# Column-major products of a four-layer decoder: two passes of 512 and 256 columns in place of three of 256

## The chip, the cores and the metric

The kernel runs as one program on one core of a Trainium2 chip. The metric is the device time of one execution in microseconds (us); a smaller number is better. The engines named below are PE (TensorE, matmuls; its weight loads have a row of their own, PEld), DVE (VectorE), ACT (ScalarE), POOL (GpSimd) and SP (SyncE, which issues the weight transfers).

## The reference

256 tokens of 1024 features pass four layers. The mixer of layer i is number i mod 3: HGRN2 (0), mLSTM (1), sliding-window attention (2), so HGRN2 comes twice, in layers 0 and 3.

```python
for layer in range(DEPTH):
    g = norm_gains[layer]
    h = x + 0.5 * swiglu(rmsnorm(x, g[0]), w_ffn_gu[layer, 0], w_ffn_down[layer, 0])
    xn = rmsnorm(h, g[1])
    ...
    h = h + mix
    h = h + 0.5 * swiglu(rmsnorm(h, g[2]), w_ffn_gu[layer, 1], w_ffn_down[layer, 1])
    gate = jax.nn.sigmoid(rmsnorm(h, g[3]) @ w_ple_gate[layer])
    x = h + gate * (p[layer] @ w_ple_proj[layer])
```

`mix` is the mixer of the layer on `xn`. `swiglu(x, w_gu, w_down)` is `(silu(g) * u) @ w_down` with `g, u` the two halves of `x @ w_gu`. `w_gu` is 1024 x 5632 and `w_down` 2816 x 1024, so the eight SwiGLU blocks hold most of the work.

## The kernel before, in words

Everything is in 32 bits. Each operand of a large product is split into two parts of 12 bits, `hi` (a cast on ACT) and `lo = x - hi` (a subtraction on DVE), and a product is the sum of three matmuls: hi.hi, hi.lo and lo.hi. Features lie on the 128 partitions, so a "feature tile" is 128 features by 256 tokens. There are 8 such tiles of the residual (KT) and 22 of the SwiGLU's middle (FT).

Weights stream from memory in units of 128 x 1024 values, two to a transfer, in the order that `weight_plan` writes out. `unit()` splits a unit on ACT and DVE (L238, L239) three units before it is used (AHEAD_UNITS), into one of six `wh` and one of six `wl` buffers. A cast therefore waits until PE has left the unit that had the buffer before.

`gemm_cols` is the column-major product: weights are the stationary operand (128 columns of a unit), activations of 256 tokens move through. For each of a unit's eight column tiles c, `mm_w` issues three matmuls of 256 columns, each with its own weight load: wh on xh, wh on xl, wl on xh (L251 to L253). Two column tiles share a PSUM bank of 512 values. The k loop is outside, so all banks of a group are done at once. The gate and up product of a SwiGLU runs in groups of four gate and four up tiles, the down product and the embedding gate (`ple`) in two halves of four tiles, the HGRN2 projection and the query and key projection of mLSTM in groups of eight. `gemm_rows` is the token-major product (L260 to L262): activations are stationary, weights move, 512 columns at a time. What reads a finished bank is DVE: in `ffn` a product by the tokens' norm `rb` (L393), SiLU on ACT, a product by the up part (L395) and a split; in `ple` L461 to L464. `push` splits a finished pair of residual tiles into `xh`, `xl` for the next product.

The work of the mixers (HGRN2's levels of decays, attention, softmax) and of the norm runs "later": generators that `tick` advances by one step per share of a unit, so their instructions stand between the products' in each engine's queue. The norm's `rb` comes after some five units of the next product. PSUM's eight banks are five for `acc`, two for `mis` and one for `out` (attention's and HGRN2's outputs). The order of the instructions on an engine is settled when the program is built, not at run time; each engine works its queue in that order.

Of the kernel before, what the change touches and what calls it, by code (L numbers as in the profile page):

```python
# [52 lines left out]

def weight_plan():
    plan = []

    def gu(l, f):
        for j in range(0, FT, 4):
            n = min(4, FT - j)
            c0, w = j * P, n * P  # L60
            cols = [(c0, w), (FF + c0, w)]
            if n == 4:
                for k in range(KT):
                    plan.append([("w_ffn_gu", (l, f), k, cols)])
            else:
                for k in range(0, KT, 2):
                    plan.append([("w_ffn_gu", (l, f), k, cols), ("w_ffn_gu", (l, f), k + 1, cols)])
# [4 lines left out]

    def halves(name, idx, nk):
        for hf in range(2):
            pairs(name, idx, hf * 512, range(nk))
# [10 lines left out]
    def ffn(l, f):  # L86
        gu(l, f)
        halves("w_ffn_down", (l, f), FT)

    for l, kind in enumerate(kinds()):  # L90
        j = (l // 3,)
        ffn(l, 0)
        if kind == 0:
            for hg in range(2):
                for k in range(KT):
                    plan.append([("hg_w_in", j, k, [(D + hg * 512, 512), (hg * 512, 512)])])
# [3 lines left out]
        elif kind == 1:  # L100
            full("ml_w_qkvo", j, 0)
# [11 lines left out]
        halves("w_ple_gate", (l,), KT)  # L113
# [3 lines left out]
class Kern:  # L117
    def __init__(self, ctx, tc, a):
# [29 lines left out]
    def s512(self, name):  # L148
        return self.tmp.tile([P, 512], F32, tag="s512", name=self.nm(name), bufs=6)

    def bank(self):
        return self.acc.tile([P, 512], F32, tag="acc", name=self.nm("acc"))
# [4 lines left out]
    def obank(self):  # L157
        return self.out.tile([P, 512], F32, tag="out", name=self.nm("out"))

# [21 lines left out]
    def settle(self, gen=None):  # L181
        """Emits all that waits, or all up to the end of gen, or until gen() holds."""
# [6 lines left out]
    def unit(self):  # L189
        """The next unit's two parts; units up to AHEAD_UNITS later are split before work that comes after."""  # L190
# [4 lines left out]
    def make_unit(self):  # L195
# [3 lines left out]
        if n % 2 == 0:  # L199
# [9 lines left out]
            elif n < 8:  # L209
                for i in range(2):  # L210
                    nc.sync.dma_start(out=self.raw[:, i, :], in_=src[:, i, :])
                if n < 6:
                    self.load_x(1 + n // 2)
            else:
                nc.sync.dma_start(out=self.raw, in_=src)
        raw = self.raw[:, n % 2, :]
        wh = self.wh.tile([P, U], F32R, tag="wh", name=self.nm("wh"))
        wl = self.wl.tile([P, U], F32R, tag="wl", name=self.nm("wl"))
        segs = self.plan[n]
        if segs[0][0] == "ml_w_out":  # L220
            # the rows' gains
# [11 lines left out]
        if n in (1, 3, 5):  # L233
            self.push(1 + n // 2)
# [11 lines left out]
    def mm_w(self, ps, w, c, x, first, last, opens):  # L246
        """ps[128 columns of w, tokens] += w[:, c:c+128].T @ x"""
# [7 lines left out]
    def mm_x(self, ps, w, c, n, x, t, first, last):  # L255
        """ps[tokens of tile t, n columns of w] += x[:, t].T @ w[:, c:c+n]"""
# [7 lines left out]
    def gemm_cols(self, x, ncol=U):  # L264
        """Column-major product over one group of ncol columns: banks of two column tiles."""
        nk = len(x)
        banks = [self.bank() for _ in range(ncol // 256)]
        per = U // ncol
        for k0 in range(0, nk, per):
            w = self.unit()  # L270
            for i in range(per):
                k = k0 + i
                for c in range(ncol // P):
                    self.mm_w(banks[c // 2][:, (c % 2) * T:(c % 2 + 1) * T], w, i * ncol + c * P, x[k],
                              k == 0, k == nk - 1, c % 2 == 0)
                self.tick(1.0 / per)
        return banks

    def gemm_rows(self, x, ncol=U):
        """Token-major product over one group of ncol columns: [t][512 columns], of half a bank if ncol is 256."""  # L280
        nk = len(x)
        if ncol == 256:
            b = self.bank()
            banks = [[b[:, t * 256:(t + 1) * 256]] for t in range(NT)]
        else:
            banks = [[self.bank() for _ in range(ncol // 512)] for _ in range(NT)]
        w = min(ncol, 512)
        per = U // ncol
        for k0 in range(0, nk, per):
            u = self.unit()  # L290
            for i in range(per):
                k = k0 + i
                for t in range(NT):
                    for n, b in enumerate(banks[t]):
                        self.mm_x(b, u, i * ncol + n * w, w, x[k], t, k == 0 and (w == 512 or t == 0), k == nk - 1)
# [888 lines left out]
```

## Time and profile before

| what | value |
|---|---|
| median of 3 runs (lowest, highest) | 2152.64 us (2149.27, 2152.68) |
| span of the profiled execution, first to last instruction | 2147.6 us |
| what lies around that span, against the median | 5.0 us |
| PE busy, PE instructions | 99% of the span, 17061 |
| DVE busy, ACT busy | 64%, 50% |
| granted TensorE clock, mean | 0.999 of 2.4 GHz |

The profile gives one execution on the chip. It does not print a run time for that execution; the three timed runs lie 1.7 to 5.1 us above its span. A matmul's row shows a start and a duration; consecutive matmuls overlap, so the spacing of their starts, and not the duration, is what one costs in a stream.

### The profile page before, as it was taken

The page shows a single profiled execution, that of the slowest core. Times are in us where ns is not written, and L with a number is a line of the kernel's source. Part 1 is how long each engine was busy: PE and PEld are TensorE (multiplying, and loading weights), DVE is VectorE, ACT ScalarE, POOL GpSimd, SP SyncE. Part 2 cuts the span into 40 slices and gives each one's busy share as a digit, 9 for nine tenths or more (in the row PEclk, how much of TensorE's full clock was granted, in tenths as well). Part 3 has the DMA queues.
Part 4 walks back from the last instruction along what each step waited for, and adds up shares of the span by engine and source line. Part 5 has one row for each costly group of instructions (what it writes and reads, how often), then busy time and mean ns, then how long its engine had stood idle before and what let it go on. Part 6 is the DMA issues. An engine that isn't in the chain of part 4 may idle for free.

```text
span 2147.6 us, 39752 instructions
## 1 busy us (share of the span) xinstructions
PE 2126.2 (99%) x17061; PEld 2078.8 (97%) x17061; DVE 1380.6 (64%) x1831; ACT 1083.4 (50%) x1442; POOL 49.1 (2%) x84
## 2 busy tenths in 40 slices
PE   8999999999999999999999999999999999999998
PEld 8999989999999989999999997899999999899998
DVE  6656986555855566665676567665576558966565
ACT  5444655443644456544454447544464445564443
POOL 2000000000000000000000001000000000000000
PEclk9999999999999999999999999999999999999999
DMA  7554344455455544454545452355554553445452
GB/s 287 180 193 177 118 160 180 179 191 181 177 184 189 180 156 163 182 190 177 188 178 184 179 195 99 123 188 181 182 183 186 177 187 129 157 155 196 177 180 77
DMA packets 54033, 372.84 MB, mean 174 GB/s; under 512 B 6368, under 2 KB 7264, under 8 KB 9568
## 3 DMA queue, kind: packets, MB, share of 16 engines
q1 hardware_dynamic: 53568, 370.21, 47.9%
q8 instruction: 133, 2.18, 0.4%
q14 instruction: 44, 0.36, 0.0%
q10 hardware_dynamic: 288, 0.09, 0.0%
HBM read 369.23 MB, written 1.05 MB: 172 GB/s over the span
## 4 chain that ended last, share of the span: by engine, by line
PE 95%; DVE 4%; ACT 1%; issue 0%; POOL 0%; DMA 0%; POOLq 0%; ACTq 0%; DVEq 0%
PE acc L252 28%; PE acc L253 28%; PE acc L251 28%; PE acc L260 2%; PE acc L261 2%; PE acc L262 2%; PE mis L625 1%; DVE slab L632 1%; PE mis L1005 1%; DVE slab L638 1%; DVE wl L239 0%; PE mis L368 0%; DVE slab L640 0%; PE mis L613 0%; DVE slab L597 0%
## 5 line engine op out<-in xcount | busy, mean ns | idle before, releaser
L239 DVE TENSOR_TENSOR wl<-wraw,wh 128x1024 fp32r<-128x1024 f32 (+1 forms) x693 | 846.1, 1222 | 620.9 <-ACT wh L238 619.5
L238 ACT CAST wh<-wraw 128x1024 fp32r<-128x1024 f32 (+1 forms) x693 | 723.7, 1046 | 950.0 <-PE acc L252 836.4
L251 PE MATMUL acc<-xh,wh 128*128 128x256 f32 x3392 | 965.0, 285 | 6.6 <-ACT xh L242 6.1
L252 PE MATMUL acc<-xl,wh 128*128 128x256 f32 x3392 | 963.0, 284 | 0.5 <-DVE xl L243 0.5
L253 PE MATMUL acc<-xh,wl 128*128 128x256 f32 x3392 | 962.5, 284 | 0.0
L251 PEld LDWEIGHTS acc<-xh,wh 128*128 128x128 f32 x3392 | 652.9, 193 | 7.0 <-ACT xh L242 6.1
L252 PEld LDWEIGHTS acc<-xl,wh 128*128 128x128 f32 x3392 | 653.0, 193 | 0.8 <-DVE xl L243 0.8
L253 PEld LDWEIGHTS acc<-xh,wl 128*128 128x128 f32 x3392 | 652.9, 193 | 0.0
L252 PE MATMUL acc<-slab,wh 128*128 128x256 f32 x1664 | 468.5, 282 | 0.0
L253 PE MATMUL acc<-slab,wl 128*128 128x256 f32 x1664 | 468.1, 281 | 0.0
L251 PE MATMUL acc<-slab,wh 128*128 128x256 f32 x1664 | 467.8, 282 | 0.1
L252 PEld LDWEIGHTS acc<-slab,wh 128*128 128x128 f32 x1664 | 313.8, 189 | 1.2 <-issue 1.0
L251 PEld LDWEIGHTS acc<-slab,wh 128*128 128x128 f32 x1664 | 313.6, 189 | 1.3 <-issue 0.8
L253 PEld LDWEIGHTS acc<-slab,wl 128*128 128x128 f32 x1664 | 313.6, 188 | 0.5 <-issue 0.3
L260 PE MATMUL acc<-wh,xh 128*128 128x512 f32 (+1 forms) x272 | 103.3, 380 | 0.0
L262 PE MATMUL acc<-wh,xl 128*128 128x512 f32 (+1 forms) x272 | 101.1, 372 | 0.0
L261 PE MATMUL acc<-wl,xh 128*128 128x512 f32 (+1 forms) x272 | 100.8, 370 | 0.0
L393 DVE TENSOR_TENSOR gs<-acc,rb 128x512 f32<-128x512 f32 x88 | 60.5, 688 | 57.7 <-PE acc L253 57.3
L394 ACT ACTIVATE gs<-gs 128x512 f32<-128x512 f32 x88 | 55.4, 630 | 19.6 <-DVE gs L393 19.5
L395 DVE TENSOR_TENSOR gs<-gs,acc 128x512 f32<-128x512 f32 x88 | 59.9, 682 | 1.2 <-ACT gs L394 0.7
L262 PEld LDWEIGHTS acc<-wh,xl 128*128 128x128 f32 x272 | 51.8, 190 | 8.7 <-issue 0.3
L260 PEld LDWEIGHTS acc<-wh,xh 128*128 128x128 f32 x272 | 51.8, 191 | 8.5 <-issue 1.3
(224 smaller groups left out, 1281.8 us busy)
## 6 DMA issues: line engine op xcount, KB each, us to landing
wraw<-in_w_all SPq DMA_DIRECT2D x346, 1024.0 KB, 4.8
wraw<-in_w_all SPq DMA_DIRECT2D x7, 512.0 KB, 7.4
pt<-in_pT SPq DMA_DIRECT2D x4, 256.0 KB, 5.0
h<-in_xT SPq DMA_DIRECT2D x3, 256.0 KB, 6.4
wraw<-in_w_all SPq DMA_DIRECT2D x2, 256.0 KB, 4.5
outT<-h SPq DMA_DIRECT2D x2, 256.0 KB, 2.1
outT<-h SPq DMA_DIRECT2D x4, 128.0 KB, 1.7
h<-in_xT SPq DMA_DIRECT2D x2, 128.0 KB, 4.5
```

The costliest lines, as they stand in the source:

```text
L238: self.nc.scalar.copy(out=hi, in_=src)
L239: self.nc.vector.tensor_tensor(out=lo, in0=src, in1=hi.bitcast(F32), op=ALU.subtract)
L251: mm(ps, wh[:, cs], xh, start=first and opens, stop=False, skip_group_check=True)
L252: mm(ps, wh[:, cs], xl, start=False, stop=False, skip_group_check=True)
L253: mm(ps, wl[:, cs], xh, start=False, stop=last, skip_group_check=True)
L260: mm(ps, xh[:, ts], wh[:, cs], start=first, stop=False, skip_group_check=True)
L261: mm(ps, xh[:, ts], wl[:, cs], start=False, stop=False, skip_group_check=True)
L262: mm(ps, xl[:, ts], wh[:, cs], start=False, stop=last, skip_group_check=True)
L393: nc.vector.tensor_tensor(out=self.two(gs), in0=self.two(g), in1=self.bc(rb), op=ALU.mult)
L394: nc.scalar.activation(gs, gs, AF.Silu)
L395: nc.vector.tensor_tensor(out=gs, in0=gs, in1=u, op=ALU.mult)
L625: nc.tensor.matmul(ps[:, i * P:(i + 1) * P], ks[:, c], qs[:, c], start=True, stop=True)
```

## The change

The parts xh and xl of a feature tile now lie side by side in one tile `x` of 512 columns. One matmul of 512 columns takes wh through both; a second of 256 columns adds wl on xh to the second half of the same bank. A column tile so fills a bank, the sum of whose halves is the result: `fold` copies one half on ACT and adds the other on DVE.

```diff
-    def mm_w(self, ps, w, c, x, first, last, opens):
...
+    def mm_t(self, ps, w, c, x, first, last):
+        wh, wl = w
+        mm = self.nc.tensor.matmul
+        cs = slice(c, c + P)
+        mm(ps, wh[:, cs], x, start=first, stop=False, skip_group_check=True)
+        mm(ps[:, T:], wl[:, cs], x[:, :T], start=False, stop=last, skip_group_check=True)
...
+def tile_order(n, nk, head):
+    return [(c, k) for k in range(nk) for c in range(head)] + [(c, k) for c in range(head, n) for k in range(nk)]
...
+    def gemm_tiles(self, x, n, head, done):
+        nk = len(x)
+        ps = {}
+        for i, (c, k) in enumerate(tile_order(n, nk, head)):
+            if i % 8 == 0:
+                w = self.unit()
+            if c // 2 not in ps:
+                ps[c // 2] = self.pair()
+            p = ps[c // 2]
+            self.mm_t(p[:, (c % 2) * 512:(c % 2 + 1) * 512], w, (i % 8) * P, x[k], k == 0, k == nk - 1)
+            if k == nk - 1:
+                done(c, p)
+            self.tick(0.125)
...
+    def fold(self, ps, out, c=0, n=2):
+        nc = self.nc
+        p4 = ps.rearrange("p (c h t) -> p c h t", c=2, h=2)[:, c:c + n]
+        o3 = out.rearrange("p (c t) -> p c t", t=T)
+        nc.scalar.copy(out=o3, in_=p4[:, :, 1, :])
+        nc.vector.tensor_tensor(out=o3, in0=p4[:, :, 0, :], in1=o3, op=ALU.add)
+        return out
```

The products that use it are gate and up (44 column tiles, `head` 4), down (8 tiles of 22 k, `head` 2), the embedding gate, both HGRN2 projections and mLSTM's queries and keys (8 tiles each, `head` 4). The first `head` tiles run with k outside; after them each tile runs all its k in a row. `weight_plan` orders the weights to match. The sums, counts and sizes of the transfers stay. `gemm_cols` with `mm_w` stays for the embedding projection, and `mm_w` in `out_proj` and mLSTM's gates.

```diff
-        self.acc = pool("acc", 5, space=PSUM)
+        self.acc = pool("acc", 3, space=PSUM)
         self.mis = pool("mis", 2, space=PSUM)
-        self.out = pool("out", 1, space=PSUM)
...
-                nc.vector.tensor_tensor(out=self.two(gs), in0=self.two(g), in1=self.bc(rb), op=ALU.mult)
+            t = self.fold(ps, self.s512("gu"))
...
+            nc.vector.tensor_tensor(out=self.two(g), in0=self.two(g), in1=self.bc(rb), op=ALU.mult)
...
-        def gates(hg, banks):
-            g, k, q, f = [self.slab() for _ in range(4)]
-            for i in range(2):
-                s = slice(i * 512, (i + 1) * 512)
-                nc.vector.tensor_tensor(out=self.two(f[:, s]), in0=self.two(banks[i]), in1=self.bc(rb), op=ALU.mult)
-                nc.vector.tensor_tensor(out=self.two(q[:, s]), in0=self.two(banks[2 + i]), in1=self.bc(rb), op=ALU.mult)
...
+        def gates(hg, f, q):
+            g, k = self.slab(), self.slab()
+            for x in (f, q):
+                x4 = x.rearrange("p (k t) -> p k t", t=T)
+                nc.vector.tensor_tensor(out=x4, in0=x4, in1=self.bc(rb, 4), op=ALU.mult)
```

The `acc` tiles are now three pairs of banks, and `out`'s work goes to `mis`. The tiles of `x`, `wh` and `wl` take 1028 values per partition instead of 512 or 1024, and the pool of 512-column scratch tiles has seven buffers instead of six. At the start of the program the four pairs of the input are loaded and pushed with units 0 to 3 instead of 0, 1, 3 and 5, since a head of four tiles takes two k from each unit.

On PE, in the gate and up product of layer 1, the order before is this (three matmuls per column tile, `acc` a bank of two column tiles, `xh` and `xl` one k):

```order
L251 MATMUL acc_6197<-xh_6097,wh_6201 128x256
L252 MATMUL acc_6197<-xl_6098,wh_6201 128x256
L253 MATMUL acc_6197<-xh_6097,wl_6202 128x256
L251 MATMUL acc_6197<-xh_6097,wh_6201 128x256
L252 MATMUL acc_6197<-xl_6098,wh_6201 128x256
L253 MATMUL acc_6197<-xh_6097,wl_6202 128x256
L251 MATMUL acc_6198<-xh_6097,wh_6201 128x256
L252 MATMUL acc_6198<-xl_6098,wh_6201 128x256
L253 MATMUL acc_6198<-xh_6097,wl_6202 128x256
```

In the change the product after its head stands so on PE (`acc` a pair of banks, `x` a pair of feature tiles, hence two k of one column tile on each):

```order
L275 MATMUL acc_5170<-x_4978,wh_5086 128x512
L276 MATMUL acc_5170<-x_4978,wl_5087 128x256
L275 MATMUL acc_5170<-x_4978,wh_5086 128x512
L276 MATMUL acc_5170<-x_4978,wl_5087 128x256
L275 MATMUL acc_5170<-x_4987,wh_5086 128x512
L276 MATMUL acc_5170<-x_4987,wl_5087 128x256
L275 MATMUL acc_5170<-x_4987,wh_5086 128x512
L276 MATMUL acc_5170<-x_4987,wl_5087 128x256
```

Three rows of 256 columns became two, of 512 and 256, and the same column tile goes on from k to k where the row before moved to the next tile.

On DVE, in the second HGRN2 projection of layer 0, before: L590 and L591 read the finished banks and multiply by `rb`, and L632 are steps of the first four heads' levels.

```order
L590 TENSOR_TENSOR slab_2943<-acc_2604,rb_2316 128x512
L632 TENSOR_TENSOR tot_2869<-tot_2824 128x16
L632 TENSOR_TENSOR slab_2584<-slab_2584,tot_2824 128x16x32
L591 TENSOR_TENSOR slab_2942<-acc_2606,rb_2316 128x512
L632 TENSOR_TENSOR slab_2585<-slab_2585,tot_2824 128x16x32
L632 TENSOR_TENSOR slab_2584<-slab_2584,tot_2869 128x8x64
L590 TENSOR_TENSOR slab_2943<-acc_2605,rb_2316 128x512
L591 TENSOR_TENSOR slab_2942<-acc_2607,rb_2316 128x512
L632 TENSOR_TENSOR slab_2585<-slab_2585,tot_2869 128x8x64
L597 TENSOR_SCALAR slab_2940<-slab_2940,omlb,lb 128x256 x2
```

In the change, at the same place: L300 are the additions of `fold`, L693 and L698 steps of the levels, L244 a weight split, L657 the products by `rb`, now on 1024 columns that lie in SBUF.

```order
L693 COPY_PREDICATED slab_1840<-mask_279,mis_2171 128x512
L698 TENSOR_TENSOR tot_2185<-tot_2143 128x64
L300 TENSOR_TENSOR slab_2067<-acc_2073,slab_2067 128x512
L693 COPY_PREDICATED slab_1841<-mask_279,mis_2177 128x512
L698 TENSOR_TENSOR slab_1846<-slab_1846,tot_2143 128x64x8
L698 TENSOR_TENSOR slab_2053<-slab_2053,tot_2143 128x64x8
L300 TENSOR_TENSOR slab_2067<-acc_2099,slab_2067 128x512
L244 TENSOR_TENSOR wl_2218<-wraw_2191,wh_2217 128x1024
...
L300 TENSOR_TENSOR slab_2068<-acc_2297,slab_2068 128x512
L657 TENSOR_TENSOR slab_2067<-slab_2067,rb_1839 128x1024
L657 TENSOR_TENSOR slab_2068<-slab_2068,rb_1839 128x1024
```

Four additions of 512 columns came in between the levels' steps, and two rows of 1024 columns follow where four of 512 stood.

On PE, at the seam from the embedding gate of layer 0 to the gate and up product of layer 1, the change puts this (`x_4978` to `x_4996` are pairs 0 to 2 of the residual's parts, `x_5051` pair 3, `acc_5062` and `acc_5071` the head's four tiles, `acc_5170` the pair after the head):

```order
L275 MATMUL acc_5170<-x_4987,wh_5086 128x512
L276 MATMUL acc_5170<-x_4987,wl_5087 128x256
L275 MATMUL acc_5170<-x_4996,wh_5086 128x512
L276 MATMUL acc_5170<-x_4996,wl_5087 128x256
L275 MATMUL acc_5170<-x_4996,wh_5086 128x512
L276 MATMUL acc_5170<-x_4996,wl_5087 128x256
L275 MATMUL acc_5062<-x_5051,wh_5058 128x512
L276 MATMUL acc_5062<-x_5051,wl_5059 128x256
L275 MATMUL acc_5062<-x_5051,wh_5058 128x512
L276 MATMUL acc_5062<-x_5051,wl_5059 128x256
L275 MATMUL acc_5071<-x_5051,wh_5058 128x512
L276 MATMUL acc_5071<-x_5051,wl_5059 128x256
```

The last two k of the head wait for pair 3, and six k of the next column tile were moved ahead of them.

## Rows read from the trace of the kernel before

**Rows 1.** the page: span, busy us by engine, granted clock, chain that ended last.

```profile
span 2147.6 us, 39752 instructions
...
PE 2126.2 (99%) x17061; PEld 2078.8 (97%) x17061; DVE 1380.6 (64%) x1831; ACT 1083.4 (50%) x1442; POOL 49.1 (2%) x84
...
PEclk9999999999999999999999999999999999999999
...
PE 95%; DVE 4%; ACT 1%; issue 0%; POOL 0%; DMA 0%; POOLq 0%; ACTq 0%; DVEq 0%
```

**Rows 2.** groups by line: count, busy us, mean ns, idle us before, releaser.

```profile
L251 PE MATMUL acc<-xh,wh 128*128 128x256 f32 x3392 | 965.0, 285 | 6.6 <-ACT xh L242 6.1 <-DVE gs L461 0.5
...
L239 DVE TENSOR_TENSOR wl<-wraw,wh 128x1024 fp32r<-128x1024 f32 (+1 forms) x693 | 846.1, 1222 | 620.9 <-ACT wh L238 619.5
L238 ACT CAST wh<-wraw 128x1024 fp32r<-128x1024 f32 (+1 forms) x693 | 723.7, 1046 | 950.0 <-PE acc L252 836.4 <-PE acc L262 45.9 <-issue 30.3
...
L251 PE MATMUL acc<-slab,wh 128*128 128x256 f32 x1664 | 467.8, 282 | 0.1
...
L395 DVE TENSOR_TENSOR gs<-gs,acc 128x512 f32<-128x512 f32 x88 | 59.9, 682 | 1.2 <-ACT gs L394 0.7
...
L446 ACT COPY pw<-acc 128x512 f32<-128x512 f32 x16 | 9.2, 588 | 1.4 <-PE acc L253 1.0
```

**Rows 3.** timeline of PE, a gate and up product, 104 rows: start, duration us.

```profile
399.81 0.28 PE L252 MATMUL acc<-xl,wh 128*128 128x256 f32 x1
...
412.17 0.28 PE L253 MATMUL acc<-xh,wl 128*128 128x256 f32 x1
```

**Rows 4.** timeline of PE, a down product, 106 rows.

```profile
524.82 0.28 PE L252 MATMUL acc<-slab,wh 128*128 128x256 f32 x1
...
537.20 0.28 PE L252 MATMUL acc<-slab,wh 128*128 128x256 f32 x1
```

**Rows 5.** timeline of PE, token-major product of layer 0, 13 consecutive 512-column rows.

```profile
261.16 0.40 PE L260 MATMUL acc<-wh,xh 128*128 128x512 f32 x1
...
263.89 0.39 PE L260 MATMUL acc<-wh,xh 128*128 128x512 f32 x1
```

**Rows 6.** windows in layer 0's HGRN2 mixer: busy us (instructions) by engine, clock.

```profile
225.00:230.00 5.00, 5.00 (x44) 5.00 (x43) 4.97 (x6) 4.97 (x9) 0.00 (x0) 1.00 0.00 0
260.00:265.00 5.00, 5.00 (x27) 4.28 (x27) 5.00 (x7) 4.96 (x11) 0.00 (x0) 1.00 0.47 143
...
300.00:305.00 5.00, 5.00 (x27) 4.27 (x26) 1.85 (x2) 3.38 (x5) 0.00 (x0) 1.00 0.59 215
```

**Rows 7.** timeline of DVE, start of the HGRN2 gates of layer 0.

```profile
224.15 0.68 DVE L590 TENSOR_TENSOR slab<-acc,rb 128x512 f32<-128x512 f32 x1
...
239.37 1.22 DVE L632 TENSOR_TENSOR slab<-slab,tot 128x1024 f32<-128x1024 f32 x1
```

**Rows 8.** timeline of ACT and DVE, end of the embedding gate of layer 0.

```profile
556.46 0.37 ACT L370 COPY rb<-mis 128x256 f32<-128x256 f32 x1 [1.35 <-PE mis L368]
556.85 1.28 ACT L462 ACT_TABLE_LOAD   x1
...
570.85 1.69 DVE L243 SCALAR_TENSOR_TENSOR xl<-h,gains,xh 128x256 fp32r<-128x256 f32 x4 [0.20 <-ACT xh L242]
```

**Rows 9.** timeline of ACT, PE and DVE around the last product.

```profile
2131.03 0.37 ACT L370 COPY rb<-mis 128x256 f32<-128x256 f32 x1 [6.92 <-PE mis L368]
...
2139.84 0.39 PE L251 MATMUL acc<-xh,wh 128*128 128x256 f32 x1 [0.52 <-DVE gs L461]
...
2143.00 0.42 DVE L461 TENSOR_TENSOR gs<-acc,rb 128x256 f32<-128x256 f32 x1 [1.79 <-PE acc L253]
...
2144.43 0.42 DVE L464 TENSOR_TENSOR h<-gs,h 128x256 f32<-128x256 f32 x1
```

**Rows 10.** waits: who waited for whom, us in total, times, longest.

```profile
ACT wh L238 <- PE acc L252: 836.4, 497, 5.6
```

**Rows 11.** the tile out: one operation's duration ns, min/median/max.

```profile
L239 DVE TENSOR_TENSOR slab<-out,slab x8: 393/420/426, 1319.1 to 1364.3; 128x256 fp32r<-128x256 f32 x8
```

More of the change, by code (lines that the diff above doesn't have):

```diff
@@ L87, in ffn @@
         gu(l, f)
-        halves("w_ffn_down", (l, f), FT)
+        tiles("w_ffn_down", (l, f), run(0, KT), FT, 2)
     for l, kind in enumerate(kinds()):
@@ L94, in weight_plan @@
             for hg in range(2):
-                for k in range(KT):
-                    plan.append([("hg_w_in", j, k, [(D + hg * 512, 512), (hg * 512, 512)])])
+                tiles("hg_w_in", j, run(D + hg * 512, 4) + run(hg * 512, 4), KT, 4)
             full("hg_w_in", j, 2 * D)
@@ L100, in weight_plan @@
         elif kind == 1:
-            full("ml_w_qkvo", j, 0)
+            tiles("ml_w_qkvo", j, run(0, 8), KT, 4)
             full("ml_w_qkvo", j, D)
@@ L112, in weight_plan @@
         ffn(l, 1)
-        halves("w_ple_gate", (l,), KT)
+        tiles("w_ple_gate", (l,), run(0, KT), KT, 4)
     return plan
@@ L148, in s512, with pair, banks @@
     def s512(self, name):
-        return self.tmp.tile([P, 512], F32, tag="s512", name=self.nm(name), bufs=6)
-    def bank(self):
-        return self.acc.tile([P, 512], F32, tag="acc", name=self.nm("acc"))
+        return self.tmp.tile([P, 512], F32, tag="s512", name=self.nm(name), bufs=7)
+    def pair(self):
+        return self.acc.tile([P, 1024], F32, tag="acc", name=self.nm("acc"))
+    def banks(self, n):
+        ps = [self.pair() for _ in range(n // 2)]
+        return [ps[i // 2][:, (i % 2) * 512:(i % 2 + 1) * 512] for i in range(n)]
     def misc(self):
         return self.mis.tile([P, 512], F32, tag="mis", name=self.nm("mis"))
-    def obank(self):
-        return self.out.tile([P, 512], F32, tag="out", name=self.nm("out"))
     def later(self, gen):
@@ L281, in gemm_rows @@
         nk = len(x)
[L282 to L286, printed above, removed]
         w = min(ncol, 512)
+        banks = self.banks(NT * ncol // w)
+        banks = [[b[:, :w] for b in banks[t * (ncol // w):(t + 1) * (ncol // w)]] for t in range(NT)]
         per = U // ncol
@@ L401, in ffn @@
[L401 to L410 removed]
+        aT = [None] * FT
@@ new lines, in ffn, with gate @@
+        todo = deque()
+        def gate(j, g, u):
+            nc.vector.tensor_tensor(out=self.two(g), in0=self.two(g), in1=self.bc(rb), op=ALU.mult)
+            nc.scalar.activation(g, g, AF.Silu)
+            nc.vector.tensor_tensor(out=g, in0=g, in1=u, op=ALU.mult)
+            s = self.slab(F32R)
+            s4 = s.rearrange("p (c h t) -> p c h t", c=2, h=2)
+            self.split(s4[:, :, 0, :], s4[:, :, 1, :], self.two(g))
+            for i in range(2):
+                aT[2 * j + i] = s[:, i * 512:(i + 1) * 512]
@@ new lines, in flush, with gated @@
+        def flush():
+            while todo:
+                gate(*todo.popleft())
+        def gated(c, ps):
+            if c % 2 == 0:
+                return
+            j = c // 4
+            t = self.fold(ps, self.s512("gu"))
+            if c % 4 == 1:
+                self.g = t
+                return
+            todo.append((j, self.g, t))
+            if len(todo) > 1:
+                self.settle(norm)
+            if norm not in self.bg:
+                flush()
+        self.gemm_tiles(x, 2 * FT, 4, gated)
@@ new lines, in ffn, with added @@
+        self.settle(norm)
+        flush()
+        self.start_norm(self.gain(l, 2 * f + 1))
+        def added(c, ps):
+            if c % 2 == 0:
+                return
+            j = c // 2
+            y = self.fold(ps, self.s512("y"))
+            nc.vector.tensor_tensor(out=self.two(y), in0=self.two(y), in1=self.bc(rb), op=ALU.mult)
+            nc.vector.scalar_tensor_tensor(out=self.h[j], in0=y, scalar=0.5, in1=self.h[j],
+                                           op0=ALU.mult, op1=ALU.add)
+            self.push(j)
@@ L415, in out_proj @@
         self.start_norm(self.gain(l, 2))
-        banks = [self.bank() for _ in range(4)]
+        banks = self.banks(4)
         for k0 in range(0, KT, 2):
```

177 lines of the change are left out of this document (78 added, 99 removed).

## The prediction

> **What bounds the kernel now.** I read the page first. PE is busy for 99% of the span of 2147.6 us, 95% of the chain that ended last is PE's, and the granted clock is at its upper level, 2.4 GHz, in every slice [rows 1]. So PE's queue sets the time nearly everywhere, and the question is what one matmul costs in a stream. Neither the busy time nor the mean duration of 285 ns [rows 2] tells that, since rows overlap; the spacing of starts in the timeline does.
>
> In a gate and up product 104 rows start between 399.81 and 412.17 us: 12.36 us over 103 steps, 120.0 ns for a matmul of 256 columns [rows 3]. In a down product it is 12.38 us over 105 steps, 117.9 ns [rows 4]. In a token-major product, matmuls of 512 columns start 2.73 us apart over 12 steps, 227.5 ns, with a weight load for each as well [rows 5]. Two of 256 columns cost 240 and one of 512 costs 227.5, so a pass costs some 12 to 13 ns beside its columns (256 columns at 2.4 GHz are 106.7 ns, 512 are 213.3).
>
> Then the groups by line and the waits say who could get in the way. DVE splits a unit in 1.22 us and ACT casts it in 1.05 [rows 2], while PE uses it in 24 x 0.120 = 2.88 us; ACT's longest wait, 836 us in sum, is for PE to release a buffer [rows 10]. So both have time in the large products. The windows show the exception: in the HGRN2 mixer DVE is busy 5.00 of 5 us from about 225 to 300 us, and falls back to 1.85 after that [rows 6].
>
> **What the change removes.** A column tile and k cost three passes of 256 before, and one of 512 and one of 256 now. The columns stay at 768, one pass goes. There are 3392 such triples on `x` and 1664 on slabs [rows 2]; 256 of the latter are `out_proj`'s (8 x 8 in four layers) and stay, so 1408 belong to the down products. Of the 3392, 128 are the second HGRN2 projections (64 in each of two layers), which run inside the DVE-bound stretch; I count nothing for them. For the other 3264: 360.0 - (227.5 + 120.0) = 12.5 ns each, 40.8 us. For the down products: 353.7 - (227.5 + 117.9) = 8.3 ns each, 11.7 us. Together 52.5 us.
>
> The trace holds no 512-column pass with weights as the stationary operand, nor one that alternates with 256. The nearest row is the token-major stream, and I take it for both. Bounds: if the 512-column pass also profits from what makes the down product 2.1 ns quicker (its operands lie in tiles of 1028 values, as all will now), a pair is 343 ns everywhere and the gain is 3264 x 17 + 1408 x 10.7 = 70.6 us. At the other end time goes by columns, 0.469 ns each as in [rows 3], and the gain is nothing.
>
> [...]
>
> **What it adds.** (1) `fold`: 243 pairs of a 512-column ACT copy out of PSUM, nearest row 588 ns, and a DVE addition with one operand in PSUM, nearest row 682 ns [rows 2]. That is 143 us of ACT and 166 us of DVE, beside PE as long as those engines keep up. In the gate and up product four column tiles (32 pairs of passes, 32 x 0.3475 = 11.1 us of PE) now bring DVE four splits and five operations of 512 columns (two additions, two products, one split), 4 x 1.22 + 5 x 0.69 = 8.3 us; ACT has 4 x 1.05 + 2 x 0.59 + 2 x 0.62 = 6.6 us. Both fit. A pair of banks is needed again two pairs later, 11 us, against a fold of 1.3 us. Cost nothing; if the cover went, it would be rival D.
>
> (2) HGRN2, where DVE is the bound. Before, the gates take four products of 512 columns out of PSUM at 0.68 us; now four additions of the same shape and two products of 1024 columns at 1.22 [rows 7], 2.44 us more for each of two head groups. The first group's first three additions fall before DVE is full, so about 2.4 + 0.4 = 2.8 us per layer, 5.6 for two. Bounds: 0, if DVE's slack after 300 us takes it back, and 2 x 4.9 = 9.8.
>
> (3) The seam from the embedding gate to the next layer. The head asks for pair 3 of `x` after 24 pairs of passes (8.3 us), where a group of eight tiles asked after 48 triples (17.3 us). From `rb`'s copy to pair 3 DVE has to do twelve operations and two additions of 512 columns at 0.68, seven push steps at 0.42 (1.69 for four [rows 8]), three splits at 1.22 and three norm sums at 0.42: 9.5 + 2.9 + 3.7 + 1.3 = 17.4 us, and about 1 us for the table load of 1.28 [rows 8] at its start: 18.4. PE has, from the same point, 24 pairs left of the gate, 24 of the head and the six that the order moved ahead: 54 x 0.3475 = 18.8 us. That is even; I take 0.5 us for each of three seams, with bounds of 0 and 3.5 (two handovers that each wait out a cast of 1.05, and a split). At the seams after down and `out_proj` no gate lies on the way: one fold, two products and the push, 5 to 6 us with a split between, against 8.3. Nothing.
>
> (4) The end. The last tile's first matmul waited 0.52 us for DVE's read of the tile before [rows 9]; that read is now a copy of 0.37 and an addition of 0.42 behind DVE's other gates. After the last matmul the same two come before the product at 2143.00. About 0.8 us each time, 1.5 in sum (bounds 0.8 and 3).
>
> (5) mLSTM and attention. `out`'s outputs share `mis`. A split of 0.42 on DVE and its cast [rows 11] hold a shared bank for about 0.8 us, eight times: bounds 0 and 6.4, I take 1, since the next user but one waits and a product's step lies between. The start: the first matmul needs xl as well as xh, which the second needed before; 0, bounds -1 and 1.
>
> **Sum.** 52.5 - 5.6 - 1.5 - 1.5 - 1.0 = 42.9 us. The span goes from 2147.6 to 2104.7. The median of the runs lies 5.0 us above the span; with the same distance the time is 2109.7, say 2110 us, against 2152.64. A measurement here tells 0.2%, some 4 us, from no change.
>
> **The rivals.**
>
> A, likeliest: as above, 2110, with 2094 to 2124 as its own range (the pass at 9 to 16 ns, side costs of 5 to 15 us). Chance 0.72.
>
> B, more: the pair at 343 ns everywhere and side costs under 8 us, 70.6 - 8 = 62 and up: 2090 and below. For it, 117.9 in [rows 4]; against it, the 227.5 of [rows 5], which no row undercuts. Chance 0.07.
>
> C, the seams give it back: the upper bounds of (2) to (5) together, 9.8 + 10.5 + 3 + 6.4 + 1 = 31, leave 22 us: 2131; with half of that excess, 2124. For it, the early need for pair 3; against it, the order's six moved pairs. Chance 0.13.
>
> D, slower: DVE takes PE's place in gate and up. It works in order, and an addition waits for ACT's copy, which can stand behind a cast: 1.05 + 0.59 + a handover of 0.1 = 1.74 us of waiting per fold at worst. DVE's 8.3 us become 8.3 + 2 x 1.74 = 11.8 for four tiles; PE took 11.5 before. Over 88 such groups that is 26 us, less the 17 us from the other products (11.7 and 448 x 12.5 ns) and plus 9.6 of side costs: about 2171. It decides from 1.6 us of waiting per fold; below 1.4 it costs nothing. Against it: other rows stand between the copy and the addition in the order. Chance 0.03.
>
> E, a pass costs nothing beside its columns in this pattern: gains of 0 to 3 ns per pair, so 0 to 14 us, less 9.6: 2162 to 2148. Against it, 227.5 is less than twice 120.0. Chance 0.05, of which 0.03 ends within 0.2% and 0.02 slower. [...]
>
> **Numbers.** Faster by over 0.2%: A, B and C, 0.92. Within 0.2%: 0.03, of E. Slower: D and the rest of E, 0.05. The range from 2088 to 2130 holds A, most of B and most of C, about 0.85.
>
> **What would show it.** In the gate and up stretch: starts in turn about 227 and 120 ns apart, 2 matmuls per 347 ns (343 would be B, 355 E). In DVE's rows: L300 near 0.69 us, DVE near 75% there and never the one that PE waits for (D). In HGRN2's windows: DVE at 5.00 for 2 to 3 us longer in each of layers 0 and 3. At the seams: a gap on PE ahead of pair 3, under 1 us (C: 3). At the end: a gap of 1.3 us or so ahead of the last tile. I would be wrong most easily on the alternating pass, which no row shows, since 1 ns there is 4.7 us.

## The result and the profile after

The kernel after takes 2123.0 us (median of four runs, 2122.7 to 2123.2) against 2151.0 for the kernel before in the same session: ratio 0.9872, interval 0.9858 to 0.9886. It is faster by 28 us, inside the range, where 43 were forecast. The span went from 2147.6 us [rows 1] to 2121.1, 26.5 less, and the steps below are held against the spans. Executions of one kernel differ in the mean granted clock of PE (in later sessions the kernel before took about 2149.5 us at 0.999 of the full clock and 2152.9 at 0.997), so where a median and a span tell different things, the span of the profile is used, with its clock.

The profile of before also holds a stretch at a granted clock of 0.50, which the page's slices [rows 1] are too coarse to show: the clock was not at 1.00 throughout. It follows a wait of PE in attention. The wait's row, and the window behind it (the granted clock is the third number from the end):

```profile
1291.46 1.11 PE L977 MATMUL mis<-ident,kd 128*128 128x128 f32 x4 [2.23 <-ACT kd L968]
```

```profile
1291.50:1294.80 3.30, 3.30 (x16) 3.30 (x17) 0.86 (x2) 3.14 (x8) 0.22 (x1) 0.50 0.00 0
```

By the starts it cost PE 1.6 us. The views give the clock as a share of its full level, in no unit. Three rows of 256 columns in that stretch:

```profile
1292.59 0.41 PE L260 MATMUL acc<-wh,xh 128*128 128x256 f32 x1
1292.80 0.41 PE L261 MATMUL acc<-wl,xh 128*128 128x256 f32 x1
1293.01 0.41 PE L262 MATMUL acc<-wh,xl 128*128 128x256 f32 x1
```

They start 213 ns apart, 1.2 columns a ns at 0.50. Twice that, 2.4 columns a ns at 1.00, is an estimate from these rows; by it 256 columns take 106.7 ns and 512 take 213.3, and the 2.4 GHz of the prediction and of the table ahead of it rests here on no more than that. The profile of after has the same wait (2.4 us by the starts, until 1273.85), keeps 1.00 behind it and has no such stretch, so 1.6 of the 26.5 us are not the change's doing.

The page of the kernel after: span, busy us by engine, shares of the chain that ended last.

```profile
span 2121.1 us, 30561 instructions
...
PE 2091.8 (99%) x12261; PEld 1825.4 (86%) x12261; DVE 1540.4 (73%) x2063; ACT 1205.0 (57%) x1678; POOL 52.7 (2%) x84
...
PE 90%; DVE 5%; issue 2%; ACT 1%; POOL 1%; DMA 0%; ACTq 0%; DVEq 0%; POOLq 0%
```

The costliest groups by line (count | busy us, mean ns | idle us before, releaser), which answer to [rows 2]:

```profile
L275 PE MATMUL acc<-x,wh 128*128 128x512 f32 x3392 | 1193.8, 395 | 8.7 <-DVE x L248 7.0
L244 DVE TENSOR_TENSOR wl<-wraw,wh 128x1024 fp32r<-128x1024 f32 (+1 forms) x693 | 844.7, 1222 | 480.1 <-ACT wh L243 478.0
...
L276 PE MATMUL acc<-x,wl 128*128 128x256 f32 x3392 | 953.1, 281 | 0.0
...
L300 DVE TENSOR_TENSOR gu<-acc,gu 128x512 f32<-128x512 f32 x176 | 120.3, 684 | 7.4 <-ACT gu L299 7.0
L299 ACT COPY gu<-acc 128x512 f32<-128x512 f32 x176 | 102.3, 581 | 16.1 <-PE acc L276 16.1
```

PE still sets the time with 4800 matmuls fewer. DVE has 160 us more work, and `fold` costs what the rows of before said: 684 ns for the addition, 581 for the copy. The durations of L275 and L276 overlap again, so the spacing tells the price. First and last rows of PE's timeline in a gate and up product (75 rows between and with these), which answer to [rows 3]:

```profile
396.82 0.39 PE L275 MATMUL acc<-x,wh 128*128 128x512 f32 x1
...
409.78 0.39 PE L275 MATMUL acc<-x,wh 128*128 128x512 f32 x1
```

In a down product (77 rows), to set beside [rows 4]:

```profile
509.70 0.39 PE L275 MATMUL acc<-slab,wh 128*128 128x512 f32 x1
...
522.97 0.40 PE L275 MATMUL acc<-slab,wh 128*128 128x512 f32 x1
```

In the token-major product of layer 0 (21 rows), to set beside [rows 5]:

```profile
257.30 0.39 PE L266 MATMUL acc<-wl,x 128*128 128x512 f32 x1
...
261.95 0.40 PE L265 MATMUL acc<-wh,x 128*128 128x512 f32 x1
```

12.96 us over 37 pairs are 350 ns a pair, 13.27 over 38 are 349, and the token-major pass, which the change did not touch but for its operands' tiles, went from 227.5 to 232.5 ns (4.65 us over 20 steps). Averaged over all distances between neighbouring starts in the trace, without those more than 30 ns off the median: 231.8 + 117.9 ns on `x`, 231.7 + 117.6 on slabs, 231.8 token-major. Such averages are used from here on.

Four lines of the waits (who waited for whom: us in total, times, longest):

```profile
PEld mis L404 <- POOL rc L374: 7.5, 13, 1.4
DVE gu L300 <- ACT gu L299: 7.0, 10, 1.3
PE acc L275 <- DVE x L248: 7.0, 1, 7.0
PE mis L404 <- POOL rc L374: 3.8, 4, 1.1
```

The third is the wait for the first input at the program's start. The first and fourth were not foreseen: PE waits at L404, where it spreads 1/rms (`rc`) over the partitions, in 13 of 16 norms. In the profile of before the same weight load (L368 there) waited twice, 1.4 us in all.

### The profile page after: what moved, and what is told of

Same layout as the page of the kernel before. It is cut to its first block, busy times and chain, and to the rows that moved or that the text cites. A ratio compares the mean times of both kernels' runs of the same rounds, so it can differ in the third digit from the quotient of the medians.

```text
span 2121.1 us, 30561 instructions
## 1 busy us (share of the span) xinstructions
PE 2091.8 (99%) x12261; PEld 1825.4 (86%) x12261; DVE 1540.4 (73%) x2063; ACT 1205.0 (57%) x1678; POOL 52.7 (2%) x84
## 4 chain that ended last, share of the span: by engine, by line
PE 90%; DVE 5%; issue 2%; ACT 1%; POOL 1%; DMA 0%; ACTq 0%; DVEq 0%; POOLq 0%
PE acc L275 51%; PE acc L276 26%; PE acc L265 2%; PE acc L267 2%; PE acc L266 2%; PE mis L691 1%; PE acc L257 1%; PE acc L256 1%; PE acc L258 1%; DVE wl L244 1%; DVE slab L698 1%; DVE slab L704 1%; PE mis L1074 1%; PE mis L404 0%; PE mis L679 0%
## 5 line engine op out<-in xcount | busy, mean ns | idle before, releaser
L275 PE MATMUL acc<-x,wh 128*128 128x512 f32 x3392 | 1193.8, 395 | 8.7 <-DVE x L248 7.0
L244 DVE TENSOR_TENSOR wl<-wraw,wh 128x1024 fp32r<-128x1024 f32 (+1 forms) x693 | 844.7, 1222 | 480.1 <-ACT wh L243 478.0
L276 PE MATMUL acc<-x,wl 128*128 128x256 f32 x3392 | 953.1, 281 | 0.0
L275 PEld LDWEIGHTS acc<-x,wh 128*128 128x128 f32 x3392 | 638.6, 188 | 156.8 <-DVE x L248 8.8
L276 PEld LDWEIGHTS acc<-x,wl 128*128 128x128 f32 x3392 | 639.6, 189 | 0.0
L275 PE MATMUL acc<-slab,wh 128*128 128x512 f32 x1408 | 492.2, 394 | 0.0
L276 PE MATMUL acc<-slab,wl 128*128 128x256 f32 x1408 | 394.2, 280 | 0.0
L275 PEld LDWEIGHTS acc<-slab,wh 128*128 128x128 f32 x1408 | 264.4, 188 | 61.3
L276 PEld LDWEIGHTS acc<-slab,wl 128*128 128x128 f32 x1408 | 265.0, 188 | 0.0
L300 DVE TENSOR_TENSOR gu<-acc,gu 128x512 f32<-128x512 f32 x176 | 120.3, 684 | 7.4 <-ACT gu L299 7.0
L299 ACT COPY gu<-acc 128x512 f32<-128x512 f32 x176 | 102.3, 581 | 16.1 <-PE acc L276 16.1
L265 PE MATMUL acc<-wh,x 128*128 128x512 f32 (+1 forms) x272 | 103.2, 381 | 0.0
L267 PE MATMUL acc<-wh,x 128*128 128x512 f32 (+1 forms) x272 | 100.6, 370 | 0.0
L256 PE MATMUL acc<-slab,wh 128*128 128x256 f32 x256 | 73.7, 289 | 0.1
L257 PE MATMUL acc<-slab,wh 128*128 128x256 f32 x256 | 72.5, 283 | 0.0
L244 DVE TENSOR_TENSOR slab<-gu,slab 128x512 fp32r<-128x512 f32 x88 | 59.9, 685 | 0.0
```

The source lines that it names most:

```text
L244: self.nc.vector.tensor_tensor(out=lo, in0=src, in1=hi.bitcast(F32), op=ALU.subtract)
L256: mm(ps, wh[:, cs], xh, start=first and opens, stop=False, skip_group_check=True)
L257: mm(ps, wh[:, cs], xl, start=False, stop=False, skip_group_check=True)
L265: mm(ps, xh[:, ts], wh[:, cs], start=first, stop=False, skip_group_check=True)
L267: mm(ps, xl[:, ts], wh[:, cs], start=False, stop=last, skip_group_check=True)
L275: mm(ps, wh[:, cs], x, start=first, stop=False, skip_group_check=True)
```

## The experiments

**The same kernel with three passes.** Order, tiles and `fold` as after, but no pass joined.

```diff
-        mm(ps, wh[:, cs], x, start=first, stop=False, skip_group_check=True)
+        mm(ps[:, :T], wh[:, cs], x[:, :T], start=first, stop=False, skip_group_check=True)
+        mm(ps[:, T:], wh[:, cs], x[:, T:], start=False, stop=False, skip_group_check=True)
         mm(ps[:, T:], wl[:, cs], x[:, :T], start=False, stop=last, skip_group_check=True)
```

> The change with its order, folds and weight plan, but three passes of 256 columns again (hi.hi into the first half of the bank, the other two into the second). This is the change's cost side alone. If the gain comes from the pass that went (350 ns for a pair of passes against some 355 to 360 for three), PE's stream grows by 4672 x 8 ns = 37 us on the changed kernel's 2123, to 2155 to 2170, above the kernel before. If the gain came from the order or the layout of the operands instead, it stays within 10 us of 2123.

Measured: 2149.2 us, ratio 0.9989 (0.9980 to 0.9999). PE's timeline in a gate and up product (104 rows):

```profile
396.77 0.28 PE L276 MATMUL acc<-x,wh 128*128 128x256 f32 x1
...
408.97 0.28 PE L277 MATMUL acc<-x,wl 128*128 128x256 f32 x1
```

12.20 us over 103 steps are 118.4 ns, where the same products took 120.0 before [rows 3]; a triple is 354.5 ns on average instead of 360. Everything except the joined pass leaves the time where it was: 3264 x 5.5 ns = 18 us from quicker passes, given away again on the way. The joined pass alone is worth the 26 us between this kernel and the one after, and 4.9 ns of each pair (354.5 to 349.6).

**Does the bank or a new `x` cost the 4 ns?** The tiles behind the head two at a time, so that neighbouring pairs change the bank (the last embedding gate keeps its order); once with the same k for both, once with k half a round apart (its line in place of the added one below).

```diff
-    return [(c, k) for k in range(nk) for c in range(head)] + [(c, k) for c in range(head, n) for k in range(nk)]
+    for c in range(head, n, 2):
+        for k in range(nk):
+            order += [(c, k), (c + 1, k)]
...
+            order += [(c, k), (c + 1, (k + nk // 2) % nk)]
```

> After the head, two column tiles at a time with k outside: the passes change bank with every pair and x with every second pair, as in the head. In the trace of the change the head has 228.8 + 118.6 ns and the rest 231.5 + 118.2. If the 2.7 ns come from staying in one bank or from a new x for every pair, the whole stream runs at 347.4 ns: 3500 pairs x 2.5 ns, 8 to 9 us less, 2114. If they come from something else in that stretch (traffic of the other engines), it stays at 2123.

> Two column tiles at a time as in the run with two tiles, but the second tile runs half of the k range apart, so that the bank changes with every pair and so does x. If the bank is the cause, 228.8 + 118.6 as in the head, 2114. If a new x for every pair is the cause, 231.5 + 118.2 as in the change, 2123.

Measured: 2120.8 us, ratio 0.9864 (0.9848 to 0.9881), spacing 231.3 + 117.7; and 2130.6 us, ratio 0.9897 (0.9883 to 0.9912), spacing 232.4 + 117.8. Neither gets near 227.5, so neither the bank nor a new moving operand makes the difference. Some 5 us of the second kernel's time are clock: its profiled execution holds a granted clock of 0.50 from 1284.8 to 1295.0 us, which cost PE 4.8 us by the starts.

**Does the alternation?** Once the second pass takes 512 columns too (it then adds the low weights times the low activations, which the kernel leaves out); once the eight long passes of a unit come first and its eight short ones behind.

```diff
-        mm(ps[:, T:], wl[:, cs], x[:, :T], start=False, stop=last, skip_group_check=True)
+        mm(ps, wl[:, cs], x, start=False, stop=last, skip_group_check=True)
```

```diff
+            for c, k, p, cs in part:
+                mm(p, wh[:, cs], x[k], start=k == 0, stop=False, skip_group_check=True)
+            for c, k, p, cs in part:
+                mm(p[:, T:], wl[:, cs], x[k][:, :T], start=False, stop=k == nk - 1, skip_group_check=True)
```

> Both passes are 512 columns wide: wl goes through xh and xl, which adds the product lo.lo to the sum. If 512-column passes cost 227.5 ns whatever stands between them, a pair is 455 ns, 105 more than now: 4672 x 0.105 = 491 us more, 2614. If a 512-column pass with weights as the stationary operand costs 231.5 by itself, 463 ns and 2651. Should alternating 512 and 256 be what adds the 4 ns, the spacing here is 227.5.

> In each unit the eight passes of 512 columns come first and then the eight of 256, into the same banks. If alternating the two lengths costs the 4 ns above the token-major 227.5, the stream is 8 x 227.5 + 8 x 118 ns and 4672 pairs save 4 ns each: 19 us less than the change's 2123, about 2105. If the passes cost what they cost in either order, 2123.

Measured: 2664.2 us, ratio 1.2384 (1.2365 to 1.2402), every 512-column pass at 231.3 to 232.2 ns. The 28 rows of PE from 499.66 us on:

```profile
499.66 0.39 PE L276 MATMUL acc<-x,wl 128*128 128x512 f32 x1
...
505.90 0.40 PE L275 MATMUL acc<-x,wh 128*128 128x512 f32 x1
```

The grouped kernel: 2139.4 us, ratio 0.9941 (0.9921 to 0.9960), 232.0 and 117.7 ns. So in these tiles 512 columns cost 231.3 to 232.2 ns beside 512, 232.0 grouped and 231.8 beside 256 in the kernel after. That the grouped one is 16 us slower than the kernel after does not come from the spacing at a granted clock of 1.00. Two of its waits of PE:

```profile
PE acc L293 <- DVE x L248: 16.1, 4, 7.2
...
PE acc L293 <- DVE gs L308: 3.4, 1, 3.4
```

Besides 7.2 us at the start, PE stands still 8.9 us at the three seams from embedding gate to next layer, for a pair of `x`, and 3.4 at the end: a unit's steps of the norm come behind all of its sixteen passes there, and the gate and the push come late by that much. Behind two of the seams, in attention and at the end the granted clock falls to 0.50:

```profile
559.00:562.30 3.30, 3.30 (x11) 2.63 (x10) 3.30 (x7) 1.20 (x3) 0.00 (x0) 0.50 0.00 0
1074.40:1077.70 3.30, 3.30 (x13) 2.94 (x12) 3.09 (x5) 1.87 (x4) 0.00 (x0) 0.50 0.00 0
1282.60:1285.90 3.30, 3.30 (x17) 3.30 (x16) 1.87 (x2) 3.20 (x8) 0.00 (x0) 0.50 0.14 20
2125.70:2132.40 6.70, 5.49 (x16) 4.42 (x16) 2.59 (x6) 0.68 (x2) 0.00 (x0) 0.50 0.37 138
```

By the starts that costs 6.7 us. With 9.4 at the seams and 2.3 more at the end than the kernel after, less 2.7 at the spreads of the norms, it makes 15.7 of the 16.5 us between the spans.

**Do the tiles' sizes?** `wh`, `wl` and `x` back to 1024 values per partition; first in the kernel after, then in the one whose passes all take 512 columns. The slabs keep 1028 in both.

```diff
-        wh = self.wh.tile([P, SLAB], F32R, tag="wh", name=self.nm("wh"))[:, :U]
+        wh = self.wh.tile([P, U], F32R, tag="wh", name=self.nm("wh"))
...
-        x = self.xs.tile([P, SLAB], F32R, tag="x", name=self.nm("x"), bufs=6)
+        x = self.xs.tile([P, U], F32R, tag="x", name=self.nm("x"), bufs=6)
```

> The tiles of wh, wl and x take 1024 values per partition again instead of 1028; all else is the change. If the spacing of 118 against the 120 before comes from where the operands lie, the passes get slower by 2 ns each, 4672 x 2 x 2 ns = 19 us more, 2142. If the stride does nothing, 2123.

> The kernel in which the second pass takes 512 columns too (it adds the low weights times the low activations, which the kernel leaves out), with the weight and x tiles back at 1024 values a row; the slabs of the down products stay at 1028. Theory A (the layout of the operands sets the few ns, and beside it nothing): every 512-column pass on x comes down to the 227 to 228.5 ns of the token-major products in that layout, those on slabs stay at 231 to 232, and the span is 2662.8 - 6784 x 3.7 ns = 2638 us. Theory B (column products cost 231 to 232 whatever the layout, because the activations move and the weights stand): 231 to 233 on both, and the span stays within 5 us of 2663.

Measured: 2122.4 us, ratio 0.9860 (0.9840 to 0.9880); token-major back at 228.6, but a pair on `x` is 232.5 + 116.3 = 348.8. This kernel's profiled execution holds a granted clock of 0.50 from 1272.9 to 1276.3 us, 1.6 us of loss that the kernel after does not have, so what its passes gained hardly shows in its time. The other, in a single execution: span 2632.2 us, 31 less than with 1028, and its 28 rows of PE from 499.68 us on:

```profile
499.68 0.39 PE L275 MATMUL acc<-x,wh 128*128 128x512 f32 x1
...
505.80 0.39 PE L276 MATMUL acc<-x,wl 128*128 128x512 f32 x1
```

6.12 us over 27 steps are 226.7 ns, where the tiles of 1028 gave 231.1 (6.24 over 27). On slabs, which did not change, it stays at 232. So in these runs the layout of the operands does set the few ns, but only in a stream of equal passes: when 512 and 256 alternate, the pair costs 348.8 in one layout and 349.6 in the other. Which of the three tiles sets it was not tried.

**What do the additions on DVE cost?** `fold` only copies one half; the other half of each sum is left out.

```diff
-        nc.scalar.copy(out=o3, in_=p4[:, :, 1, :])
-        nc.vector.tensor_tensor(out=o3, in0=p4[:, :, 0, :], in1=o3, op=ALU.add)
+        nc.scalar.copy(out=o3, in_=p4[:, :, 0, :])
```

> The fold only copies the first half of each bank on ACT: the addition of the second half on DVE is left out, and with it the hi.lo and lo.hi terms of the sum. 166 us of DVE go. If DVE's additions are covered, as forecast, except in HGRN2 and at the seams, 5 to 8 us go: about 2116. If DVE holds PE up all along, much more, 30 us and up. If they cost nothing anywhere, 2123.

Measured: 2119.3 us, ratio 0.9852 (0.9836 to 0.9867): 158 us of DVE's work taken out gain 3.7 us. Its profiled execution holds two stretches at a granted clock of 0.50 (from 41.5 and from 1273.7 us), 3.1 us of loss that the kernel after's does not have, so about 6 us would be the gain at the same clock, as an estimate from the spans. PE's stalls in HGRN2 do not shrink: 4.0 us in layer 0 and 3.2 in layer 3, where the kernel after has 3.8 and 2.9. Of the kernel's stalls, those at the norm behind each of the three seams are gone, and that says more than the sum. The seam behind layer 0 in the kernel after, all engines:

```profile
570.93 0.50 PE L399 MATMUL mis<-ones,ss 128*128 128x1 f32 x4
571.54 0.16 DVE L373 TENSOR_SCALAR rc<-mis 128x2 f32<-128x2 f32 x1 [0.20 <-PE mis L399]
571.62 3.49 DVE L244 TENSOR_TENSOR wl<-wraw,wh 128x1024 fp32r<-128x1024 f32 x3
571.78 1.61 POOL L374 TENSOR_TENSOR rc<-rc,mhalf 128x2 f32<-128x2 f32 x1 [24.63 <-DVE rc L373]
573.45 0.71 PE L404 MATMUL mis<-ident,rc 128*128 128x128 f32 x4 [1.08 <-POOL rc L374]
```

And without the additions:

```profile
574.30 0.15 DVE L372 TENSOR_SCALAR rc<-mis 128x2 f32<-128x2 f32 x1
574.53 0.69 POOL L373 TENSOR_TENSOR rc<-rc,mhalf 128x2 f32<-128x2 f32 x1 [25.56 <-DVE rc L372]
575.28 0.71 PE L403 MATMUL mis<-ident,rc 128*128 128x128 f32 x4
...
576.24 1.23 DVE L244 TENSOR_TENSOR wl<-wraw,wh 128x1024 fp32r<-128x1024 f32 x1 [1.79 <-ACT wh L243]
```

The norm's power on GpSimd took 0.70 us, but 1.61 where DVE began a split 0.16 us ahead of it: that is so in four norms of the kernel after (the three seams and mLSTM's), in none of before, and these are the four in which PE's matmul itself waited, in the fourth line of the waits.

**The shared banks.** The kernel before, with `out`'s outputs in `mis`.

```diff
-        return self.out.tile([P, 512], F32, tag="out", name=self.nm("out"))
+        return self.misc()
```

> The kernel before, with the outputs of attention and HGRN2 in the two mis banks instead of a bank of their own; nothing else is changed. The change's attention, with its output projection, takes 106.1 us against 103.0 before. If the shared banks are the reason, attention grows by 2 to 3 us here, and the time from 2151 to 2154; if not, it stays at 103.

Measured: 2156.7 us, ratio 1.0026 (1.0011 to 1.0041), at a mean granted clock down to 0.994. The profiled span, at 0.999, is 2149.5 us, 1.9 more than before, with the same stretch at 0.50 in attention. HGRN2's stalls are the same to 0.1 us. Two new ones stand in attention:

```profile
1345.50 0.48 PE L1004 MATMUL mis<-slab,slab 64*128 64x128 f32 x2 [0.18 <-DVE slab L1006]
...
1347.19 0.65 PE L1043 MATMUL mis<-pT,s 128*64 128x256 f32 x4 [0.73 <-ACT pT L1037]
```

PE lost 0.40 and 0.89 us ahead of these, by the starts: 1.3 us for the sharing.

**The spread of 1/rms half a unit later.** Four pairs of passes lie between the sum of squares and the spread; now eight.

```diff
-W_SQ, W_SS, W_RC = 1.0, 0.5, 0.5
+W_SQ, W_SS, W_RC = 1.0, 0.5, 1.0
```

> The kernel after the change, with the two products that spread 1/rms over the partitions issued eight pairs of passes behind the products that sum the squares, where it was four. Theory (the new seam cost is this wait: after the change TensorE stands 1.24 us ahead of the spread at the three seams from embedding gate to next layer and 0.68 us at the mLSTM's norm, because rc comes out of DVE's queue and GpSimd's 1.61 us power too late): the four gaps go, 3 x 1.24 + 0.68 = 4.4 us, so 2123.0 - 4.4 = 2118.6 us. Rival (the wait only moves, since the gates that need the broadcast come 1.4 us later too): the gaps stand before the next product instead, 2122 to 2125 us.

Measured: 2122.9 us, ratio 0.9874 (0.9859 to 0.9889): nothing gained. All sixteen spreads now start without a wait. But the embedding gate's norm is later as well, and this is the seam that its result must reach:

```profile
554.16 0.28 PE L276 MATMUL acc<-x,wl 128*128 128x256 f32 x1
...
555.40 1.66 DVE L248 SCALAR_TENSOR_TENSOR x<-h,gains,x 128x256 fp32r<-128x256 f32 x4
...
556.02 0.47 PE L275 MATMUL acc<-x,wh 128*128 128x512 f32 x1 [1.58 <-DVE x L248]
...
570.39 1.61 POOL L374 TENSOR_TENSOR rc<-rc,mhalf 128x2 f32<-128x2 f32 x1 [24.22 <-DVE rc L373]
...
572.20 0.60 PE L404 MATMUL mis<-ident,rc 128*128 128x128 f32 x4
```

PE loses 1.7 us by the starts at each of three seams for pair 3 of `x`, and 3.5 + 0.4 at the end where it had lost 1.6: 7.4 us, for the 6.5 that the spreads no longer cost. Right behind the wait at the end the granted clock is 0.50 from 2110.8 to 2114.2 us, and the passes there lose 1.2 us more. Their starts:

```profile
2111.56 0.41 PE L276 MATMUL acc<-x,wl 128*128 128x256 f32 x1
2111.77 0.63 PE L275 MATMUL acc<-x,wh 128*128 128x512 f32 x1
2112.20 0.41 PE L276 MATMUL acc<-x,wl 128*128 128x256 f32 x1
```

**Versions that put the gains together.** Two tiles at a time with the later spread, and the same with tiles of 1024.

> The kernel that takes the tiles behind the first four two at a time (2120.8 us), with the spread of 1/rms eight pairs behind the sum of squares. If the norm's wait and the order of tiles are separate causes, their gains add: 2120.8 - 4.4 = 2116.4 us. If the order already hides part of the wait: 2118 to 2121 us.

> The same with the weight and x tiles at 1024 values a row, where a pair of passes on x took 348.8 ns against 349.6 and the token-major 512-column passes 228.5 against 231.8. 3392 x 0.8 ns = 2.7 us and about 600 x 3.3 ns = 2.0 us: 2116.4 - 4.7 = 2111.7 us if these rows decide; 2115 to 2117 us if other waits take it back, as with the change of stride alone, which gained 0.6 us.

Measured: 2124.6 us, ratio 0.9882 (0.9866 to 0.9898), and 2124.6 us, ratio 0.9887 (0.9870 to 0.9903). No better than the kernel after. Their intervals overlap with those of the kernel after, of two tiles at a time and of the tiles of 1024, so none here is shown to beat it. Both carry the later spread's wait at the end, with a granted clock of 0.50 behind it (1.4 us of loss each); their profiled spans are 2118.7 and 2121.5 us. Whether the gains add at one clock stays open.

## Why the prediction was right, and where it was short

**The sign and the mechanism hold.** PE was the bound, a pass fewer in each pair is what gained (2149.2 to 2123.0 by the first experiment), and the covers for `fold` held. Rival D is out: the addition waited 7.0 us for its copy in all, 1.3 at most, below the 1.6 from which it would decide; the handover of 0.1 in D's sum was the author's estimate (the last addition below starts 0.04 us behind its copy). Rival E is out by the first experiment: no run shows its 0 to 3 ns a pair, the joined pass alone gave 4.9. Rival B is out too, since no pair came near 343. C came true in part, but not where it was placed. Its sum has a slip: half of the excess leaves 52.5 - (9.6 + 10.7) = 32 us, 2120 and not 2124, so the 2123 measured lies in C's reach as well as in A's.

**The step that was mis-sized is the pair.** It was put at 227.5 + 120.0 on `x` and 227.5 + 117.9 on slabs, a gain of 52.5 us. It measured 349.6 and 349.3. 3264 x (360.0 - 349.6) + 1408 x (354.6 - 349.3) = 33.9 + 7.5 = 41.4 us, 11.1 short. The forecast took the price of a pass beside its columns, 12 to 13 ns, from two rows of one layout [rows 3, 5] and used it in another and in a pattern that no row showed. In the layout of after, 118.1 for 256 columns and 231.8 for 512 leave 4.4 ns a pass; 120.0 before and the 226.8 of the tiles of 1024 leave 13.

**The side costs** were put at 9.6 us. The spans say 41.4 - 26.5 = 14.9, and 1.6 more that before lost at a granted clock of 0.50 and after did not: 16.5. By the starts of PE's rows, before against after:

- (1) `fold` in the large products: nothing, as forecast.
- (2) HGRN2: stalls over 0.25 us went from 2.8 to 3.8 us in layer 0 and from 2.4 to 2.9 in layer 3. 1.5 us, not 5.6. DVE is busy 5.00 us of 5 from 220 to 235 us, as forecast, but PE's stalls grew by less than DVE's work, and taking the additions out did not shorten them. So the step from added work on DVE to added time is not borne out; what made the stalls grow stays open.
- (3) The seam: pair 3 was in time, with no wait in the kernel after. The forecast called it even (18.4 against 18.8 us), and the later spread shows that it was: half a unit (1.4 us) more turned into 1.7 us of waiting.
- (4) The end: the last tile's wait went from 0.7 to 1.6 us by the starts, and from the start of the last matmul to the product by `rb` it was 0.31 us before (2142.69 to 2143.00) and is 1.23 now. 0.9 each time, 1.8 together, where 1.5 were forecast. The wait's row names the tile's read, as forecast, and the rows behind the last matmul show copy and addition:

```profile
2112.54 0.50 PE L275 MATMUL acc<-x,wh 128*128 128x512 f32 x1 [1.40 <-DVE gs L300]
...
2115.34 0.28 PE L276 MATMUL acc<-x,wl 128*128 128x256 f32 x1
2115.70 0.37 ACT L299 COPY gs<-acc 128x256 f32<-128x256 f32 x1 [1.83 <-PE acc L276]
2116.11 0.42 DVE L300 TENSOR_TENSOR gs<-acc,gs 128x256 f32<-128x256 f32 x1 [1.30 <-ACT gs L299]
2116.57 0.42 DVE L517 TENSOR_TENSOR gs<-gs,rb 128x256 f32<-128x256 f32 x1
```

- (5) Attention: its stalls over 0.25 us went from 3.6 to 5.9 us, 2.3, of which the shared banks explain 1.3 by the experiment; what makes the rest was not tried. mLSTM lost 0.3 less than before. 2.0 together, not 1. The start cost 0.8, by the starts from the 20th pair on.
- Not in the forecast: the norms. `tick` came after a whole or half unit before and comes after an eighth now, so the spread follows the sum of squares by four pairs, 1.4 us, where 1.9 to 3.3 us lay between their starts in the norms of before that did not wait. With DVE's reading of the sum, the power and the handovers it came to 2.2 to 2.5 us in the 13 norms of after that waited. 6.5 us in 13 norms against 1.3 before: 5.2 us. That they are this wait is shown by the later spread, which ended all of them; where the gain went, by its seams.
- Not in the forecast: 624 token-major passes at 231.8 instead of 228.4 ns, 2.1 us, from the tiles of 1028.

1.5 + 1.8 + 2.0 + 0.8 + 5.2 + 2.1 = 13.4 of the 16.5; three us in small pieces stay open. What stays open too is why a pair that alternates ignores the layout that sets the price of equal passes.

**The forecast time is nearer than its steps by luck.** The pair is 11.1 us short and the side costs 6.9 too low, but two things hid 4.7 of it: the stretch at 0.50 in the profile of before, 1.6, and the 5.0 us put between span and time. Those 5.0 compare one execution's span with the median of others; the executions of the two profiles take 1.7 to 1.9 us more than their own spans.

## What to carry to other kernels

What a matmul costs beside its columns is read from a stream of the same shape, operands and layout as the one to be built; a line through two rows of different streams gave 12.5 ns where 4.9 were to be had. When work between the steps of a product is issued in finer portions, a chain over three engines that lies between two of these steps needs its distance counted again. And a wait that is covered by issuing its producer's reader later moves everything behind that reader: look first which seam has no slack. Before two times are compared, read the granted clock behind the longer waits of each profile.

## What the runs showed of the hardware

In the kernel after, GpSimd's power on 128 x 2 values took 0.70 to 0.72 us in twelve norms and 1.61 in the four in which DVE had begun a split of 128 x 1024 (`wl<-wraw,wh`) 0.16 us before it. That split ends 1.22 - 0.16 = 1.06 us into the power, which takes 1.61 - 0.70 = 0.91 longer: as an estimate from these numbers, about a wait for its end. No row names what held the power. One of the twelve ran beside an addition of 128 x 512 (`gu<-acc,gu`), begun 0.17 us before it, and took 0.72. The other way round no wait shows: in the kernel before, eleven splits that DVE began 0.35 to 0.43 us into a power took 1.22 to 1.23 us, where the mean of all is 1.22.

The price of a pass differed with the layout of its operands: 226.8 ns for 512 columns with weights and `x` in tiles of 1024 values, 231.5 in tiles of 1028, and the other way round for 256 columns, 120.0 (in the kernel before, with `xh` and `xl` in tiles of 512) against 118.1. Alternating passes gave 232.5 + 116.3 in the first and 231.8 + 117.9 in the second.

In the kernel with the later spread the passes at a granted clock of 0.50 start 426 and 214 ns apart (rows from 2111.56 us). At 1.00 the passes of the kernel after start 231.8 and 117.9 ns apart, 18.8 and 10.9 more than half of that. The clock fell there behind a wait of PE of 3.5 us, in the kernel before behind one of 2.4; the kernel after waited 2.4 us at the same place and kept 1.00.
